# Delta rule on quarters of TensorE's array: the two halves taking turns, and turns by tokens as products with the unit matrix

## The chip, the cores and the metric

The kernel runs on one core of one Trainium2 chip. The metric is device time in microseconds (us) of one execution. A core has five engines that work side by side, each through its own queue of instructions in order: TensorE (PE in the profile; its weight loads are PEld), VectorE (DVE), ScalarE (ACT), GpSimd (POOL) and SyncE (SP), which issues the large transfers. They meet at semaphores.

## The reference

Two transformer-like layers run on 256 tokens of 1024 channels. The first has block attention, a pooling mixer, and a feed-forward part with a short convolution. The second has a convolution branch and an RWKV-7 branch side by side, and then a layer of 16384 small experts. The change is in the RWKV-7 branch: 8 heads of 64 channels, each with a 64 x 64 state that a delta rule updates token by token:

```python
    def step(state, inp):
        r_t, k_t, v_t, w_t, kk_t, a_t = inp
        sa = jnp.einsum('bhij,bhj->bhi', state, -kk_t)
        state = (state * w_t[:, :, None, :]
                 + sa[..., None] * (kk_t * a_t)[:, :, None, :]
                 + v_t[..., None] * k_t[:, :, None, :])
        y_t = jnp.einsum('bhij,bhj->bhi', state, r_t)
        return state, y_t
    ...
    mean = jnp.mean(y, axis=-1, keepdims=True)
    var = jnp.mean(jnp.square(y - mean), axis=-1, keepdims=True)
    y = ((y - mean) * lax.rsqrt(var + GN_EPS)).reshape(B, S, RWKV_CH) * gn_w.astype(F32) + gn_b.astype(F32)
```

## The kernel before

Activations lie with channels on the 128 partitions and tokens along the row. The large products (`linear`, lines 312 to 315) take weights of 128 x 128 in two parts, high and low, against 256 tokens in two parts: 24 matmuls for 1024 input channels. Weights come in pieces of 1 MB (`fetch`), ScalarE copies the high part (line 205) and VectorE subtracts the low part (line 207).

The RWKV branch is worked in four chunks of 64 tokens. A tile `m` of 128 partitions is two heads: partitions 0 to 63 and 64 to 127, the two halves. All products of one head with one chunk are 64 x 64 with 64 rows, so each uses one quarter of the array: the upper left one for the first half, the lower right one for the second. They are in plain fp32, which the trace shows as two records for each matmul.

`quads(f)` calls `f` for the eight pairs of a half `h` and an index `c` of 0 to 3. The result of a set of eight lands in one PSUM tile of two banks (`two_banks`), where `c // 2` is the bank and `c % 2` the place in it. Four functions use it:

- `heads(m)`, for m of 0 to 3, makes the matrices of the keys for the four chunks (line 1100) and inverts a triangular matrix for each of the eight pairs in five levels. A level has a set of eight products (line 1125), ScalarE's copy to `X` (line 1127), a second set (line 1131), VectorE's subtraction (line 1132) and VectorE's transpose (line 1134): 40 sets in all.
- `values2(m)` turns the values and the keys by tokens (`turn4`) and makes three products for each pair (line 1185): 24 matmuls in one call of `quads`, four calls.
- `chunks()` is the chain over the four chunks. Here `c` of `quads` is the tile `m`. A chunk has one product set for `G`, one for `U` and one for the next state `S`, and the output set `Y`, which has two matmuls for each pair from the second chunk on (line 1209). Two or three matmuls on zeros (`warm`, line 382) stand ahead of each set.
- `group_norm` normalises a chunk's output on VectorE and ScalarE and turns it with `turn4`.

`turn4` turns eight 64 x 64 blocks: in the first half as TensorE transposes (line 1144), in the second as products with the unit matrix (line 1146). There are 16 turns: four of `heads`, eight of `values2`, four of `group_norm`.

The heads' steps and the taps of the convolution branch (line 1287, on VectorE) are put between the projections by a small clock of due times (`at`, `tick`, `flow`). That sets the program's order. Within block 2 the compiler's scheduler then places the instructions of every engine by its own estimate of when each can run, so the order on an engine is not that of the text, and it changes when an instruction's estimated length changes.

Of the kernel before, what the change touches and what calls it, by code (L numbers as in the profile page):

```python
# [22 lines left out]
C = 64  # L23
# [150 lines left out]
class Kern:  # L174
# [711 lines left out]
    def quads(self, f):  # L886


        for h in range(2):
            for c in range(4):  # L890
                f(c, slice(64 * h, 64 * h + 64), c // 2, c % 2)

    def by4(self, p):

# [242 lines left out]
    def turn4(self, p, src):  # L1137

        te, ident = self.nc.tensor, self.c("ident")

        def turn(c, h, b, i):
            out = p[h, b, i * C:i * C + C]
            if h.start == 0:
                te.transpose(out, src(c, h), ident[h, h])
            else:
                te.matmul(out, src(c, h), ident[h, h], start=True, stop=True)

        self.quads(turn)

    def values2(self, m):  # L1150

# [554 lines left out]
```

## Time and profile before

| | |
|---|---|
| Runs before, median of 3 | 1444.72 us (1439.47 to 1444.98) |
| Profiled execution, own time | 1444.46 us |
| Its span, first to last instruction | 1442.7 us |
| PE busy over the span | 1400.3 us (97%) |
| DVE, ACT, POOL busy | 1110.6, 719.0, 269.6 us |
| Mean granted clock of TensorE | 0.979 of full speed (2.4 GHz) |

The first product on a quarter of the array starts at 447.4 us, the last at 586.3 us. Busy time of PE counts each matmul from its start to the modelled end of its pipeline; a matmul of the next instruction starts long before that, so 97% is not a share of what the array can do. What a stretch of matmuls costs is therefore read from starts in the timeline: merged rows give the first start and the time to the last end. A granted clock of 0.5 is the lower of TensorE's two levels, 1.2 GHz.

### The profile page before, as it was taken

To read this page: it belongs to the slowest core of one execution; us is meant where nothing else is said; L and a number is where in the kernel's file an instruction comes from. 1 tells how busy PE (TensorE), PEld (TensorE's weight loads), DVE (VectorE), ACT (ScalarE), POOL (GpSimd) and SP (SyncE) were. 2 spreads that over 40 slices of the span, in tenths; PEclk is the share of its full clock that TensorE was granted. 3 is DMA by queue.
4 is the path that set the end of the run, shared out by engine and by line. 5 is a ranking of instruction groups with operands and counts; after the bars stand their busy time and mean duration, and the time that the engine had idled before them with its cause. 6 is when DMAs were issued, how large, how long until landed. Compare 5 with 4: busy or idle time off the path is not lost. (4 is left out here: it accounts for less than half of the span.)

```text
span 1442.7 us, 27290 instructions
## 1 busy us (share of the span) xinstructions
PE 1400.3 (97%) x11208; PEld 1284.6 (89%) x11208; DVE 1110.6 (77%) x1967; ACT 719.0 (50%) x1079; POOL 269.6 (19%) x242
## 2 busy tenths in 40 slices
PE   9999999999869999989998999999999999999997
PEld 7889999999868897989998999999987777888886
DVE  5779999994598875769978867878679999655555
ACT  5576566564674333554453544434454444444443
POOL 1800032220285210022456440000000000000000
PEclk8999999999989998999999999999999999999999
DMA  7568867862413110364544555445555556654552
GB/s 282 196 199 295 295 220 266 273 221 88 161 59 112 37 60 2 117 212 168 179 172 147 205 175 176 164 160 176 172 209 174 187 199 230 206 201 175 196 184 88
DMA packets 40446, 253.83 MB, mean 176 GB/s; under 512 B 4736, under 2 KB 4992, under 8 KB 13440
## 3 DMA queue, kind: packets, MB, share of 16 engines
q1 hardware_dynamic: 38592, 246.79, 49.5%
q10 hardware_dynamic: 1728, 5.28, 1.1%
q8 instruction: 88, 1.44, 0.4%
q14 instruction: 38, 0.31, 0.1%
HBM read 249.96 MB, written 2.10 MB: 175 GB/s over the span
## 5 line engine op out<-in xcount | busy, mean ns | idle before, releaser
L205 ACT CAST whi<-raw 128x1024 fp32r<-128x1024 f32 (+1 forms) x418 | 435.1, 1043 | 498.5 <-PE psu L313 219.7
L207 DVE TENSOR_TENSOR wlo<-raw,whi 128x1024 fp32r<-128x1024 f32 (+1 forms) x389 | 488.3, 1259 | 197.1 <-ACT whi L205 196.1
L312 PE MATMUL psu<-u3hi,whi 128*128 128x256 f32 x1128 | 285.6, 286 | 4.4 <-DVE qe L520 4.4
L313 PE MATMUL psu<-u3lo,whi 128*128 128x256 f32 x1128 | 281.3, 283 | 0.0
L312 PEld LDWEIGHTS psu<-u3hi,whi 128*128 128x128 f32 x1128 | 214.5, 190 | 4.6 <-DVE qe L520 4.6
L313 PEld LDWEIGHTS psu<-u3lo,whi 128*128 128x128 f32 x1128 | 214.2, 190 | 0.0
L315 PE MATMUL psu<-u3hi,wlo 128*128 128x256 f32 x1128 | 180.9, 282 | 4.0 <-DVE wlo L207 2.9
L315 PEld LDWEIGHTS psu<-u3hi,wlo 128*128 128x128 f32 x1128 | 154.4, 189 | 5.2 <-DVE wlo L207 3.3
L1394 PE MATMUL acc<-whi,u3hi 128*128 128x512 f32 x504 | 140.8, 399 | 0.0
L1394 PE MATMUL acc<-whi,u3lo 128*128 128x512 f32 x504 | 138.2, 394 | 0.0
L1394 PE MATMUL acc<-wlo,u3hi 128*128 128x512 f32 x504 | 138.2, 394 | 0.0
L1394 PEld LDWEIGHTS acc<-wlo,u3hi 128*128 128x128 f32 x504 | 94.7, 188 | 22.3
L1394 PEld LDWEIGHTS acc<-whi,u3lo 128*128 128x128 f32 x504 | 94.7, 188 | 22.0
L1394 PEld LDWEIGHTS acc<-whi,u3hi 128*128 128x128 f32 x504 | 92.2, 188 | 19.1
L207 POOL TENSOR_TENSOR wlo<-raw,whi 128x1024 fp32r<-128x1024 f32 x29 | 72.0, 2483 | 190.5 <-ACT whi L205 190.5
L312 PE MATMUL mm<-u3hi,whi 128*128 128x256 f32 (+1 forms) x312 | 82.3, 295 | 0.0
L313 PE MATMUL mm<-u3lo,whi 128*128 128x256 f32 (+1 forms) x312 | 78.7, 284 | 0.0
L313 PE MATMUL mm<-flo,whi 128*128 128x256 f32 x272 | 67.6, 282 | 0.0
L312 PE MATMUL mm<-fhi,whi 128*128 128x256 f32 x272 | 67.6, 282 | 0.0
L312 PEld LDWEIGHTS mm<-u3hi,whi 128*128 128x128 f32 x312 | 59.5, 191 | 3.2 <-issue 2.5
L312 PE MATMUL mm<-n3hi,whi 128*128 128x256 f32 (+1 forms) x160 | 48.3, 326 | 14.0 <-DVE kr L960 9.4
L313 PEld LDWEIGHTS mm<-u3lo,whi 128*128 128x128 f32 x312 | 59.5, 191 | 0.3 <-issue 0.2
(432 smaller groups left out, 2599.4 us busy)
## 6 DMA issues: line engine op xcount, KB each, us to landing
raw<-in_w_fm SPq DMA_DIRECT2D x74, 1024.0 KB, 4.9
raw<-in_peer_u SPq DMA_DIRECT2D x64, 1024.0 KB, 4.8
raw<-in_peer_v SPq DMA_DIRECT2D x64, 1024.0 KB, 4.9
ada<-in_ada_w SPq DMA_DIRECT2D x40, 512.0 KB, 5.3
raw<-in_w_qkv SPq DMA_DIRECT2D x5, 1024.0 KB, 10.4
H<-in_ada_w SPq DMA_DIRECT2D x8, 512.0 KB, 3.9
raw<-in_w_qkv SPq DMA_DIRECT2D x4, 256.0 KB, 5.3
xd<-kr SPq DMA_DIRECT2D x1, 1024.0 KB, 9.9
```

What stands on the lines that cost most here:

```text
L205: self.nc.scalar.copy(hi, src)
L207: e.tensor_tensor(lo, src, hi.bitcast(F32), op=OP.subtract)
L312: mm(out, w[k][0], x[k][0], start=start and k == 0, stop=False)
L313: mm(out, w[k][0], x[k][1], start=False, stop=False)
L315: mm(out, w[k][1], x[k][0], start=False, stop=stop and k == n - 1)
L1394: mm(acc[a], w[:, tt * 128:tt * 128 + 128], v[:, dh * 512:dh * 512 + 512], start=start, stop=stop)
```

## The change

`quads` runs over the same eight pairs, but the halves take turns, and the second half is two indices ahead: (first, 0), (second, 2), (first, 1), (second, 3), (first, 2), (second, 0), (first, 3), (second, 1). So the two halves mostly write different banks. `turn4` has no transposes any more: both halves are products with the unit matrix.

```diff
     def quads(self, f):
 
 
-        for h in range(2):
-            for c in range(4):
-                f(c, slice(64 * h, 64 * h + 64), c // 2, c % 2)
+        for n in range(8):
+            h = n % 2
+            c = (n // 2 + 2 * h) % 4
+            f(c, slice(64 * h, 64 * h + 64), c // 2, c % 2)
...
-        def turn(c, h, b, i):
-            out = p[h, b, i * C:i * C + C]
-            if h.start == 0:
-                te.transpose(out, src(c, h), ident[h, h])
-            else:
-                te.matmul(out, src(c, h), ident[h, h], start=True, stop=True)
-
-        self.quads(turn)
+        self.quads(lambda c, h, b, i: te.matmul(p[h, b, i * C:i * C + C], src(c, h), ident[h, h], start=True, stop=True))
```

The count of instructions stays: 680 matmuls on quarters, 10388 in all. Line numbers of the changed kernel are one higher from line 892 to `turn4`, and six lower after it. The scheduler moves instructions on PE, DVE and ACT; POOL's and SP's order stays. Groups of quarter products between full-size ones are 51 where they were 50.

In the first levels of `heads` PE has, before (1125 and 1131 are the two sets of a level, `keep` is the unit matrix, 312 to 315 are projections):

```order
L1125 MATMUL two<-lora,Alv 64x64 x8
L312 MATMUL mm<-n3hi,whi 128x256
L313 MATMUL mm<-n3lo,whi 128x256
L312 MATMUL mm<-n3hi,whi 128x256
L1125 MATMUL two<-lora,Alv 64x64 x8
L1144 MATMUL two<-keep,beb_4547 64x64 x4
L1146 MATMUL two<-keep,beb_4547 64x64 x4
L313 MATMUL mm<-n3lo,whi 128x256
L312 MATMUL mm<-n3hi,whi 128x256
L1131 MATMUL two<-eL,X 64x64 x8
L313 MATMUL mm<-n3lo,whi 128x256
L1131 MATMUL two<-eL,X 64x64 x8
```

And with the change:

```order
L1126 MATMUL two<-lora,Alv 64x64 x8
L1109 MATMUL sm<-bonus,cst 128x256
L1126 MATMUL two<-lora,Alv 64x64 x8
L1142 MATMUL two<-keep,beb_4547 64x64 x8
L1132 MATMUL two<-eL,X 64x64 x16
L312 MATMUL mm<-n3hi,whi 128x256
L313 MATMUL mm<-n3lo,whi 128x256
```

The single projections between the sets move behind them, and the turn is eight products of one kind.

In the chain over the chunks VectorE has, before (1218 copies half of `U`, which PE needs for the next state; 1345 is the reciprocal of the convolution branch's norm):

```order
L1224 TENSOR_TENSOR G<-two,sg 128x256
L1261 TENSOR_TENSOR Y<-Y,ysm 128x256
L1345 RECIPROCAL cvr<-cvr 128x256
L1264 TENSOR_REDUCE ysm<-yq 128x4
L1218 COPY U<-two 128x128
```

And with the change:

```order
L1218 TENSOR_TENSOR G<-two,sg 128x256
L1255 TENSOR_TENSOR Y<-Y,ysm 128x256
L1258 TENSOR_REDUCE ysm<-yq 128x4
L1212 COPY U<-two 128x128
L395 RECIPROCAL ysm<-ysm 128x4
L1260 TENSOR_TENSOR Y<-Y,ysm 128x256
L1339 RECIPROCAL cvr<-cvr 128x256
```

The reciprocal stood ahead of the copy of `U` and now stands behind it.

## Rows read from the trace of the kernel before

**Rows 1.** The profile's page, busy time of each engine over the span

```profile
PE 1400.3 (97%) x11208; PEld 1284.6 (89%) x11208; DVE 1110.6 (77%) x1967; ACT 719.0 (50%) x1079; POOL 269.6 (19%) x242
```

**Rows 2.** Busy time by stretch: PE, PEld, DVE, ACT, POOL, granted clock, DMA share

```profile
420.00:440.00 20.00, 14.68 (x80) 14.24 (x81) 18.95 (x27) 13.33 (x24) 15.53 (x16) 0.66 0.15 54
440.00:543.00 103.00, 101.60 (x1318) 91.92 (x1316) 81.93 (x169) 37.40 (x78) 28.39 (x32) 1.00 0.18 63
543.00:590.00 47.00, 45.00 (x460) 37.17 (x460) 28.29 (x76) 17.52 (x38) 1.50 (x2) 0.85 0.07 24
560.00:580.00 20.00, 18.40 (x164) 15.08 (x164) 10.11 (x29) 7.70 (x16) 0.00 (x0) 0.66 0.00 1
```

**Rows 3.** Waits of PE, 440 to 500: us in total, times, longest

```profile
PE two L1125 <- DVE lora L1120: 1.2, 2, 1.1
```

**Rows 4.** Waits of DVE, 440 to 500

```profile
DVE lora L1120 <- POOL eL L1118: 4.1, 4, 1.3
DVE eL L1132 <- PE two L1131: 3.1, 5, 1.2
DVE cvy L952 <- PE mm L315: 1.9, 1, 1.9
```

**Rows 5.** Waits of DVE, 500 to 543

```profile
DVE eL L1132 <- PE two L1131: 7.0, 5, 2.4
DVE QE L1173 <- PE sm L1170: 3.1, 2, 2.8
```

**Rows 6.** Timeline of PE, 407.8 to 408.4: start, us to the last end

```profile
408.15 0.38 PE L1015 MATMUL two<-lr,lora 64*128 64x256 f32 x1
408.15 0.38 PE L1016 MATMUL two<-lr,lora 64*128 64x256 f32 x1
408.37 0.38 PE L1015 MATMUL two<-lr,lora 64*128 64x256 f32 x1
```

**Rows 7.** Timeline of PE, 512.6 to 513.4, where one set follows another

```profile
512.70 0.22 PE L1125 MATMUL two<-lora,Alv 64*64 64x64 f32 x1
512.75 0.22 PE L1185 MATMUL two<-kp,QE 64*64 64x64 f32 x1
512.76 0.22 PE L1125 MATMUL two<-lora,Alv 64*64 64x64 f32 x1
...
513.05 0.34 PE L1185 MATMUL two<-kp,QE 64*64 64x64 f32 x3
```

**Rows 8.** Timeline of PE, a turn and sets of a level, 447 to 478

```profile
447.36 0.41 PE L1144 MATMUL two<-keep,beb 64*64 64x64 f32 x4
447.70 0.68 PE L1146 MATMUL two<-keep,beb 64*64 64x64 f32 x8
...
471.31 1.54 PE L1131 MATMUL two<-eL,X 64*64 64x64 f32 x32
473.09 0.96 PE L1131 MATMUL two<-eL,X 64*64 64x64 f32 x16
475.49 2.46 PE L1125 MATMUL two<-lora,Alv 64*64 64x64 f32 x48
```

**Rows 9.** Busy time by stretch of line 1125, line 1131 (440 to 500) and line 1185

```profile
440.00:500.00 60.00, 12.69 (x240) 11.38 (x240) 1.00 0.21 72
440.00:500.00 60.00, 11.84 (x224) 10.55 (x224) 1.00 0.21 72
500.00:520.00 20.00, 2.83 (x48) 2.69 (x48) 1.00 0.16 54
```

**Rows 10.** Timeline of all engines, 559 to 563, in the chain

```profile
559.68 1.75 DVE L1345 RECIPROCAL cvr<-cvr 128x256 f32<-128x256 f32 x1 [1.05 <-ACT cvr L1344]
561.63 0.28 DVE L1218 COPY U<-two 128x128 f32<-128x128 f32 x1
561.96 0.49 PE L382 MATMUL two<-zero 128*128 128x256 bf16 x3 [1.60 <-DVE U L1218]
562.38 0.96 PE L1209 MATMUL two<-U,tb 64*64 64x64 f32 x16
```

## The prediction

> **What bounds the kernel now.** I read the page's busy times first, then a table by stretch, the waits of PE and of DVE in the stretch that holds the quarter products, and last the timeline of PE there. PE is busy 97% of the span [rows 1], so a saving on PE is worth something wherever PE does not wait. The reader should see where that holds: from 440 to 543 us PE is busy 101.6 of 103 us at the full clock, 2.4 GHz, with DVE at 81.9 [rows 2], and PE's only wait of note is 1.2 us [rows 3]. Just before, from 420 to 440, it is the other way round: DVE is busy 18.95 of 20 us, PE 14.68, and the granted clock averages 0.66 [rows 2]. From 440 on DVE waits for PE instead: 5.0 us up to 500, mostly on the second set of a level [rows 4], and 10.1 us from 500 to 543 [rows 5]. So PE sets the pace of heads and values, with DVE not far behind. From 543 to 590, the chain over the chunks, neither is full (45.0 and 28.3 of 47 us) [rows 2]; there results go round between PE, ACT and DVE.
>
> **What two halves do at once.** The trace already has places where matmuls of the two halves stand side by side. Lines 1015 and 1016 read the upper and the lower 64 rows, alternate in program order, and start together: two at 408.15, and the next 0.22 us later [rows 6]. For quarters, the end of one set beside the start of the next shows it: the second half's last records of line 1125 at 512.70 and 512.76 with the first half's record of line 1185 at 512.75 between them [rows 7]. Within one half a record follows the other after 0.06 us ((0.34 - 0.22) / 2, the three records at 513.05 [rows 7]). So two records, one of each half, take the 0.06 us that one takes now. With strict turns nearly a whole set should run so, where today only about three records at each border do.
>
> **Part 1: the 40 sets of the levels.** A set is 16 records and takes 0.96 us alone, two 1.54, three 2.46 [rows 8]. As eight pairs it takes seven steps of 0.06, one first step that is 0.05 longer, and the 0.22 of the last record: 0.69. Two sets take 15 steps, 1.17; three take 23, 1.65. The savings are 0.27, 0.37 and 0.81, per set 0.27, 0.19 and 0.27. I take 0.25: 40 x 0.25 = 10.0 us of PE. Of 640 records 464 lie before 500 us [rows 9], so 7.3 fall there and 2.7 after.
>
> **Part 2: the 24 products of each of the four calls of values.** Such a call is 48 records and takes 2.83 us [rows 9]. By turns of three matmuls it would be 23 steps and 0.27, 1.65 us, if TensorE takes the other half's matmuls while one half has two in hand, as the border at 512.7 suggests. 1.2 x 4 = 4.8 us, all after 500.
>
> **Part 3: the turns.** Now four transposes start at 447.36, and the second half's products start only at 447.70 and end 0.68 later, at 448.38 [rows 8]. As 16 records in pairs the turn should take the 0.69 of a set, so it ends at 448.05: 0.33 saved, four times before 500 (1.3), eight up to 543 (2.6), four in the chain (1.3). A rule speaks against this part. The Trainium skill, "Perfetto Trace Analysis", section Transposes, says that a logical transpose should be a transpose and not a standard matmul, since it skips the arithmetic. The rows agree in that four transposes take 0.41 and four products 0.68. By that rule 16 turns would cost 16 x 0.27 = 4.3 us more instead of 5.2 less, and the sum below would lose 9 of its PE time. I do not follow it, since the second half's products now stand behind the first half's and would stand beside them.
>
> **What of it shows, 440 to 543.** PE would need 7.3 + 1.3 = 8.6 us less before 500, and 2.7 + 4.8 + 2.6 = 10.1 less after. What DVE can give is its waits on PE: 5.0 before 500 and 10.1 after [rows 4, 5]; its 4.1 us of waits on POOL stay [rows 4]. The lower of the two in each piece is 5.0 and 10.1, 15.1 us. That is the most, if each wait vanishes and no new one comes. The least is nothing, if DVE's order binds at once. With both engines nearly full and results passing back and forth, some of either's time is lost in new waits; I take three quarters, 11.3 us. What is late next is DVE: 81.9 us of work against some 92 us of stretch.
>
> **The chain, 543 to 590.** It has eleven single sets, three double ones (16 matmuls, 32 records) and four turns. Singles save 0.27 each (3.0). A double saves 16 steps of 0.06 less the three that its halves share at their border today, 0.78 each (2.3). Turns 1.3. Together 6.6 us of PE time, of which I count half, 3.3, because sets stand both on the round of results and beside it (PE's waits for ACT and DVE take the rest). To that comes the moved reciprocal: it holds DVE for 1.75 us from 559.68, the copy of U ends behind it, and PE waits 1.60 for U [rows 10]. In the new order it stands behind that copy, so 1.6 us go. Against it stands the clock: from 560 to 580 the granted clock averages 0.66, so 20 x 0.34 / 0.5 = 13.6 us at the lower level, 1.2 GHz, at a place where PE had idled [rows 2, 10]. With shorter sets PE is idle for a larger share. If the lower level lasts as long again, it costs 6.8 us of full-clock work; bounds are 0 and 6.8, and I take 1.0, as at the lower level a set in pairs takes about what a set takes now at the upper. The chain gives 3.3 + 1.6 - 1.0 = 3.9 us.
>
> **The other edits.** One more group of quarter products (51 for 50) means two more switches between quarter and full-size matmuls. No row shown has a switch alone; the nearest is the step from transposes to products inside a turn, from 447.36 + 0.41 - 0.22 = 447.55 to 447.70, 0.15 us [rows 8]. Two cost between nothing and 0.3; I take 0.1, within the rounding. POOL's and SP's order stays. After 590 nothing changes, and PE is the engine that is full there too, so what is gained is carried to the end.
>
> **Sum.** 11.3 + 3.9 = 15.2 us. From the profiled execution's 1444.46 us (span 1442.7 and 1.8 around it, 0.3 below the median of the runs, 1444.72) that is 1429.3; I say 1429.
>
> **Rivals.**
> *PE's saving shows in full.* If DVE's overlapping instructions leave it more room than its busy time says, all of 8.6 + 10.1 + 6.6 + 1.6 = 26.9 us go: 1418. For it: DVE's instructions start before the previous one's end. Against: DVE was the late engine until 440.
> *DVE takes over at once.* Taps and low parts stand in DVE's order between the steps of the levels; where PE is early it waits behind them. Then 440 to 543 gives 4 and the chain 2: 1438.5. For it: DVE at 80% and the backlog from before 440. Against: it waited 15 us on PE.
> *The clock falls in the levels: slower.* If PE's waits on DVE between 440 and 543 become like those from 420 to 440 (5.3 idle in 20 us, clock 0.66), each 20 us loses 20 x 0.34 = 6.8 us of full-clock work. Three such stretches cost 20.4: 1449.7, slower than before. It decides from 15.2 / 6.8 = 2.2 stretches on. Against: PE's idle share by the sum is under 10 of 92 us. The Trainium skill, "TensorE: Matmul & The Clock Gate", section "A second HAM failure mode", describes just such a throttling through short idle times between groups of matmuls; here 440 to 543 runs at 1.00 with groups as short as eight matmuls.
> *The halves do not run side by side.* Then the sets stay, and turns lose 16 x 0.27 = 4.3 less the hole of some 0.1 ahead of the second half (1.6): 1447. Rows 6 and 7 speak against it.
>
> **How the numbers follow.** Forecast 0.57, PE in full 0.16, DVE at once 0.17, clock 0.05, no turns 0.05. The forecast's own range is 1422 to 1436. What a measurement can tell from no change is 0.5%, 7.2 us: faster means below 1437.2 or so. Forecast 0.56 faster and 0.01 same; PE in full 0.16 faster; DVE at once 0.07 faster, 0.10 same; clock 0.02 same and 0.03 slower; no turns 0.03 same and 0.02 slower. Faster 0.79, same 0.16, slower 0.05. The range, 1418 to 1440, leaves out half of PE in full, a sixth of DVE at once and nearly all of the last two: 0.2.
>
> **What would show it.** Right: a set of 16 records merged in under 0.75 us where it took 0.96; a call of values near 1.65; a turn near 0.7 with no hole; DVE's waits on line 1131's sets mostly gone; the last quarter product before 574. Wrong: records of the two halves that start 0.06 apart instead of together (no turns); PE waits on DVE of more than 8 us from 440 on (DVE at once); a granted clock below 0.9 between 440 and the start of the chain (clock).

## The result and the profile after

The changed kernel takes 1421.73 us, median of 6 runs (1417.35 to 1423.11), where the kernel before took 1440.03 beside it on the same chip (6 runs, 1439.47 to 1444.98). The ratio is 0.9857, 95% interval 0.9835 to 0.9878: 20.6 us less by the ratio, 18.3 by the medians. Forecast were 1429.0 us and 15.2 us less. So the change made the kernel faster as forecast, inside the range, by 5 us more than the sum had it (3 by the medians); and the gain sits elsewhere than the sum put it, which is the matter of this text.

The page of the kernel after has PE's busy time 31 us below [rows 1]. It still fills 97% of the span:

```profile
span 1417.0 us, 27418 instructions
...
PE 1369.4 (97%) x11272; PEld 1258.2 (89%) x11272; DVE 1111.3 (78%) x1967; ACT 718.8 (51%) x1079; POOL 270.7 (19%) x242
```

To see where the time went, I cut each trace at three marks: the first quarter product, the last record of the values, and the last turn by tokens. Between the first two lie heads and values ("the head" below), between the last two the chain. Busy time by stretch, of the kernel before: the first 40 us, head, chain, and the piece of the chain at the lower clock (us, then PE, PEld, DVE, ACT, POOL, granted clock, DMA share, GB/s):

```profile
0.00:40.00 40.00, 37.14 (x173) 29.96 (x174) 22.07 (x43) 21.00 (x33) 7.68 (x13) 0.87 0.74 275
447.40:542.40 95.00, 93.60 (x1251) 84.34 (x1251) 75.10 (x155) 32.16 (x68) 28.39 (x32) 1.00 0.16 57
542.40:586.30 43.90, 41.90 (x437) 33.85 (x435) 26.05 (x71) 16.68 (x36) 1.50 (x2) 0.84 0.03 7
563.50:577.20 13.70, 13.70 (x103) 10.98 (x101) 5.76 (x17) 5.71 (x13) 0.00 (x0) 0.50 0.01 2
```

The same of the kernel after, with two short pieces of its head:

```profile
0.00:40.00 40.00, 36.97 (x192) 29.71 (x192) 27.32 (x51) 24.88 (x39) 12.82 (x19) 1.00 0.86 320
442.20:528.50 86.30, 79.06 (x1298) 70.91 (x1297) 76.63 (x157) 31.77 (x68) 29.26 (x32) 0.96 0.19 63
528.50:560.30 31.80, 29.79 (x454) 23.95 (x452) 25.01 (x70) 16.86 (x36) 1.45 (x2) 1.00 0.04 7
469.60:473.00 3.40, 3.40 (x37) 3.17 (x39) 3.40 (x9) 0.23 (x1) 0.17 (x1) 0.50 0.00 0
496.90:500.30 3.40, 3.40 (x52) 3.06 (x51) 3.40 (x8) 0.78 (x3) 0.00 (x0) 0.50 0.26 39
```

The head gave 8.7 us (95.0 to 86.3) and the chain 12.1 (43.9 to 31.8). What follows the chain is the same length: 1442.7 - 586.3 = 856.4 before, 1417.0 - 560.3 = 856.7 after. The remaining 5.2 us of the two spans' difference lie ahead of the first quarter product (447.4 to 442.2): the profiled execution of before has a piece at the lower clock in its first 40 us (0.87), that of after has none. The change touches nothing there, and an experiment with the same code up to that point, the kernel before with the reciprocal cut, has no such piece and its first quarter product at 442.3; so it is not counted as the change's. 8.7 + 12.1 - 0.3 = 20.5, the 20.6 of the ratio.

The steps themselves are what the sum said. Timeline of PE after, two sets of line 1132 (line 1131 before) and the last turn:

```profile
464.15 1.15 PE L1132 MATMUL two<-eL,X 64*64 64x64 f32 x32
...
468.82 0.68 PE L1132 MATMUL two<-eL,X 64*64 64x64 f32 x16 [2.98 <-DVE eL L1133]
...
471.55 2.38 PE L1126 MATMUL two<-lora,Alv 64*64 64x64 f32 x48
...
559.87 0.68 PE L1142 MATMUL two<-keep,Y 64*64 64x64 f32 x16
560.48 0.39 PE L313 MATMUL mm<-u3lo,whi 128*128 128x256 f32 x1
```

A set of 16 records takes 0.68 us for 0.96 [rows 8] (forecast 0.69), two sets 1.15 for 1.54 (1.17), a turn 0.68 without a hole for 1.02 (0.69). The 48 records at 471.55 take 2.38, where 1.65 was forecast, since they run at the clock of 0.50 up to 473.0. For two calls of the values, 96 records (line 1179; 1185 before):

```profile
500.00:520.00 20.00, 3.46 (x96) 3.29 (x96) 0.99 0.27 102
```

1.73 us a call for 2.83 [rows 9], where 1.65 was forecast. So the halves do run beside each other, for as long as a whole set.

What PE no longer needs it partly waits for. Waits of PE, kernel after, 440 to 500 us (us in total, times, longest), which answer to [rows 3]:

```profile
PE two L1132 <- DVE eL L1133: 4.7, 2, 3.0
PE two L1126 <- DVE lora L1121: 2.3, 2, 1.4
PE two L1126 <- DVE eL L1133: 0.2, 1, 0.2
```

7.2 us instead of 1.2. The largest is the 2.98 at 468.82 above; DVE's timeline just before it, kernel after:

```profile
464.74 0.95 DVE L1281 SCALAR_TENSOR_TENSOR cvacc<-cvy,vec,cvacc 128x256 f32<-128x256 f32 x1
465.72 0.42 DVE L1091 TENSOR_TENSOR beb<-av,eN 64x256 f32<-64x256 f32 x1
...
466.91 1.52 DVE L1281 SCALAR_TENSOR_TENSOR cvacc<-cvy,vec,cvacc 128x256 f32<-128x256 f32 x3
468.35 0.75 DVE L1133 TENSOR_TENSOR eL<-eL,two 128x256 f32<-128x256 f32 x2
```

The two sets end at 465.30, and the subtraction that empties them (line 1133) starts at 468.35: three taps of the convolution (line 1281) and what is queued before them stand between, without a gap. On the other side DVE's waits for PE shrink. Waits of DVE, kernel after, 440 to 500, for [rows 4]:

```profile
DVE lora L1121 <- POOL eL L1119: 4.6, 4, 1.3
DVE eL L1133 <- PE two L1132: 1.5, 2, 1.2
DVE cvy L953 <- PE mm L315: 0.5, 1, 0.5
```

And from 500 to 529, for [rows 5]:

```profile
DVE eL L1133 <- PE two L1132: 1.6, 1, 1.6
DVE QE L1167 <- PE sm L1164: 0.5, 1, 0.5
```

5.0 became 2.0 and 10.1 became 2.1.

### The profile page after: what moved, and what is told of

It is laid out like the page before. It is cut to its first block, busy times and chain, and to the rows that moved or that the text cites. A ratio compares the mean times of both kernels' runs of the same rounds, so it can differ in the third digit from the quotient of the medians.

```text
span 1417.0 us, 27418 instructions
## 1 busy us (share of the span) xinstructions
PE 1369.4 (97%) x11272; PEld 1258.2 (89%) x11272; DVE 1111.3 (78%) x1967; ACT 718.8 (51%) x1079; POOL 270.7 (19%) x242
```

## The experiments

Three theories went in, A, B and C in the expectations. The first is the prediction's: the shorter sets and turns are the gain, in the head up to what DVE can give, and in the chain with the wait for U gone. The second: it is the end of the transposes that keeps the clock up in the chain. The third: in the head DVE has become the bound, and what relieves DVE there gives more. All results in one table; head and chain are cut at the same marks as above, in one execution of each kernel, and "low" is the time at the granted clock of 0.50 in each. Each ratio is to executions of the kernel before beside that run.

| run | ratio to before | head us | low | chain us | low |
|---|---|---|---|---|---|
| before | 1 | 95.0 | 0 | 43.9 | 13.7 |
| after | 0.9857 (0.9835 to 0.9878) | 86.3 | 6.8 | 31.8 | 0 |
| order only | 0.9943 (0.992 to 0.9965) | 94.5 | 3.4 | 36.6 | 0 |
| turns only | 0.9945 (0.9927 to 0.9962) | 95.4 | 3.4 | 37.0 | 0 |
| after, fewer taps | 0.981 (0.9789 to 0.983) | 82.1 | 0 | 33.3 | 3.4 |
| before, fewer taps | 0.9992 (0.998 to 1.0005) | 95.4 | 0 | 44.0 | 13.7 |
| before, reciprocal cut | 0.9948 (0.9926 to 0.997) | 95.1 | 0 | 37.1 | 0 |
| after, one bank | 0.9861 (0.9838 to 0.9884) | 86.4 | 6.8 | 31.9 | 0 |
| after, one warming matmul | 0.9876 (0.984 to 0.9912) | 84.9 | 3.4 | 37.5 | 6.8 |
| after, taps off DVE | 0.9925 (0.9898 to 0.9951) | 93.4 | 10.2 | 32.1 | 0 |
| after, reciprocal cut | 0.9858 (0.9837 to 0.9878) | 86.5 | 6.8 | 31.9 | 0 |
| after, low parts on POOL | 0.991 (0.9894 to 0.9927) | 91.6 | 10.2 | 33.9 | 3.4 |
| after, both of these | 0.9919 (0.99 to 0.9937) | 91.5 | 10.2 | 32.4 | 0 |
| after, again | 0.984 (0.9818 to 0.9862) | 86.4 | 6.8 | 31.8 | 0 |

**The new order alone.** The kernel before with `quads` of the kernel after; turns stay transposes in the first half and products in the second.

```diff
-        for h in range(2):
-            for c in range(4):
-                f(c, slice(64 * h, 64 * h + 64), c // 2, c % 2)
+        for n in range(8):
+            h = n % 2
+            c = (n // 2 + 2 * h) % 4
+            f(c, slice(64 * h, 64 * h + 64), c // 2, c % 2)
```

> Halves take turns in quads; the turns by tokens keep transposes in the first half, as before. Theory A (the gain is the side-by-side run of the two halves): 40 sets, values and the chain's sets gain as in the changed kernel (a set 0.68 us), turns lose their 16 x 0.33 = 5 us of PE time; 1424 to 1430 where before is 1440 and the changed kernel 1421. Theory B (the transposes are what hurts: they break the row of products and the clock falls in the chain): 1432 to 1438, with a stretch at 1.2 GHz in the chain again. Theory A expects no such stretch only if density is the cause; it leaves that open.

It took 1435.46 us (ratio 0.9943): slower than theory A's range, and in the range of the second theory (B), but without the stretch at 1.2 GHz in the chain that B forecast. Next to nothing of the gain comes from the head (94.5 for 95.0); the chain gives it (36.6 for 43.9). Timeline of PE, a set and a turn of this kernel:

```profile
462.08 0.68 PE L1126 MATMUL two<-lora,Alv 64*64 64x64 f32 x16
462.69 0.24 PE L1145 MATMUL two<-keep,beb 64*64 64x64 f32 x1
462.86 0.33 PE L1147 MATMUL two<-keep,beb 64*64 64x64 f32 x2
463.12 0.24 PE L1145 MATMUL two<-keep,beb 64*64 64x64 f32 x1
...
464.14 0.33 PE L1147 MATMUL two<-keep,beb 64*64 64x64 f32 x2
464.40 0.38 PE L313 MATMUL mm<-n3lo,whi 128*128 128x256 f32 x1
```

The sets have their 0.68, but the turn now runs from 462.69 to 464.47, 1.78 us for 1.02 [rows 8]. Each step between a transpose and a product takes 0.17 to 0.26 us from start to start, and nothing runs beside it. Twelve turns in the head lose 12 x 0.76 = 9.1 us, most of what sets and values save on PE there (12.7 us: the 16.8 found below, less 12 x 0.34 for the turns). Of the 3.6 us left, the 3.4 us at the lower clock take up to 1.7, and PE's idle time in the head grows by 1.4.

**The turns alone.** The kernel after with the order of before.

```diff
-        for n in range(8):
-            h = n % 2
-            c = (n // 2 + 2 * h) % 4
-            f(c, slice(64 * h, 64 * h + 64), c // 2, c % 2)
+        for h in range(2):
+            for c in range(4):
+                f(c, slice(64 * h, 64 * h + 64), c // 2, c % 2)
```

> Turns by tokens are products with the unit matrix in both halves; quads keeps its old order, all of the first half and then the second. Theory A: a turn takes the 0.96 us of a set where it took 1.02, so nothing is gained or lost: 1438 to 1442, sets still 0.96 us. Theory B (transposes hold the clock down in the chain): the stretch at 1.2 GHz from 563 to 577 goes and with it 6.8 us: 1432 to 1435. By the rule that products cost more than transposes: 1444.

1433.48 us (0.9945), again nothing in the head, with 3.4 us of it at the lower clock. The time is the one that B forecast. Timeline of PE, its first turn:

```profile
447.40 0.96 PE L1141 MATMUL two<-keep,beb 64*64 64x64 f32 x16
448.30 0.39 PE L313 MATMUL mm<-n3lo,whi 128*128 128x256 f32 x1
```

0.96 for 1.02: products in place of transposes cost nothing even in the old order, since the hole between the two kinds goes with them. All that this kernel wins it wins in the chain (37.0, none of it at the lower clock). Its order of DVE is another there: the long reciprocal stands behind the copy of U, as in the kernel after, and PE has no wait for U.

The two parts alone win 0.5 and -0.4 us in the head, together 8.7. Neither showed a gain in it without the other; the lower clock hides up to 1.7 us of each.

**Fewer taps on DVE, after and before.** Both leave out 28 of the 30 taps that this loop adds for one of the convolution's four tiles, some 10 us of DVE in the head.

```diff
-        for j in range(30):
+        for j in range(2 if m == 1 else 30):
```

> The changed kernel with 28 of the 30 VectorE taps of one of the convolution's four channel tiles left out (the one whose taps run between 450 and 500 us): DVE has 28 x 0.4 = 11 us less to do there, PE the same. Theory C (after the change DVE sets the pace of the levels): the stretch from the first quarter product to the last product of values, 86.3 us, gets 5 us shorter or more, and the time falls by 4 to 9 us. Theory D (PE still sets the pace, or the round of results): less than 2 us.

> The kernel before with the same 28 taps left out. Theory C (PE set the pace of the levels before): 0 to 2 us faster than before, the stretch of 95.0 us stays above 93. Theory D (DVE or the round of results set it already): the same gain as in the changed kernel with these taps left out.

In the kernel after the head goes to 82.1, 4.2 less where theory C asked for 5 or more, and the time to 1415.67; in the kernel before nothing moves (0.9992). (The profiled execution of after with fewer taps is the slowest of its four, 1421.16; it has 10.2 us at the lower clock in its first 40.) The head's row of after with fewer taps:

```profile
447.50:529.60 82.10, 76.83 (x1300) 68.51 (x1299) 66.01 (x129) 31.79 (x68) 28.93 (x32) 1.00 0.19 66
```

And of before with fewer taps:

```profile
445.20:540.60 95.40, 94.12 (x1251) 84.69 (x1251) 65.14 (x129) 32.18 (x68) 27.50 (x32) 1.00 0.17 57
```

DVE's 10 us are worth nothing before and 4.2 us after: 2.0 as less idle time of PE (7.2 to 5.3), and 2.2 as PE's work, all at the full clock here. PE's row at the full clock, 76.83, tells what its saving in the head is: 93.60 - 76.83 = 16.8 us. The rest of the head of after follows: its idle time grew from 1.4 to 7.2 us (86.30 - 79.06), which takes 5.8, and the two pieces at 0.50 make its work 2.2 longer (79.06 - 76.83): 16.8 - 5.8 - 2.2 = 8.8. In the chain of the fewer-taps kernel the reciprocal stands ahead of the copy of U again, PE waits 1.9 us for it, and 3.4 us run at the lower clock: 33.3 for 31.8.

**The reciprocal in four pieces, in the kernel before.** DVE can do other work between the pieces.

```diff
-        nc.vector.reciprocal(rs, rs)
+        for i in range(0, T, 64):
+            nc.vector.reciprocal(rs[:, i:i + 64], rs[:, i:i + 64])
```

> The kernel before with the convolution norm's reciprocal of 256 columns cut into four of 64, so that only the first, about 0.45 us, stands ahead of the copy of U that PE waits for. Theory E (the stall of 1.75 us on DVE is what idles PE, and the clock falls behind it): the stretch at 1.2 GHz in the chain goes, the chain shrinks from 43.9 to 36 or 37 us, 1433 to 1436, as with the turns alone. Theory B (the transposes hold the clock down): only the 1.3 us of the stall go, the stretch at 1.2 GHz stays, 1438 to 1441.

1435.5 us (0.9948, 7.5 us less), with the same products and transposes as before; some full-size products and DVE's list behind the copy of U stand in another order. Its chain by stretch:

```profile
537.40:574.50 37.10, 36.04 (x436) 29.42 (x435) 25.89 (x74) 16.93 (x36) 1.50 (x2) 1.00 0.04 9
```

and DVE's timeline in it:

```profile
555.12 0.36 DVE L1264 TENSOR_REDUCE ysm<-yq 128x4 f32<-128x256 f32 x1
555.40 0.28 DVE L1218 COPY U<-two 128x128 f32<-128x128 f32 x1
555.60 0.54 DVE L1346 RECIPROCAL cvr<-cvr 128x64 f32<-128x64 f32 x1
```

The copy of U slips in between two pieces, PE's wait for it falls from 1.6 to 0.4, and the clock stays at 1.00 where it had been 0.50 for 13.7 us. Chain 43.9 to 37.1. The transposes are all there, as they are in the order alone, and so the second theory is not needed for the clock.

**Both halves into one bank.** In the kernel after the two halves work at the same time on different banks of PSUM; here on the same one, in its other 64 partitions.

```diff
-            c = (n // 2 + 2 * h) % 4
+            c = n // 2
```

> The changed kernel without the second half's offset of two indices (c = n // 2): both halves of a pair write the same PSUM bank at the same time, on different partitions. If the bank can take two halves' results at once: a set stays 0.68 us and the time 1418 to 1423. If it makes them take turns: a set goes back toward 0.96 us, and the time to 1430 or more.

No difference: ratio 0.9861, and a set, from the timeline of PE:

```profile
529.73 0.68 PE L1203 MATMUL two<-sg,eL 64*64 64x64 f32 x16
```

The Trainium skill, "TensorEngine Tiling (Array Packing)", section Restrictions and Gotchas, says that different row tiles can't access the same PSUM bank at once. This trace shows no cost of it, 0.68 us for a set on one bank as on two, for two halves that write different partitions; the measurement decides. So the offset of two in `c` isn't where the gain comes from.

**One warming matmul instead of three** ahead of each set of the chain that waits (line 382 multiplies zeros).

```diff
-WARM_CHAIN = 3
+WARM_CHAIN = 1
```

> The changed kernel with one matmul on zeros ahead of each set of the chain instead of three. Theory F (they lie in waits, and the chain's round of results sets the pace): within 1 us of the changed kernel, unless the clock falls in the chain, which costs up to 7 us. Theory G (the chain is bound by PE's own row of matmuls now): 14 sets x 0.22 = 3 us faster.

The chain is 37.5 us for 31.8. Its second half by stretch:

```profile
545.00:565.00 20.00, 17.70 (x213) 15.40 (x209) 13.47 (x36) 13.74 (x22) 0.00 (x0) 0.83 0.13 45
```

6.8 us of it at the lower clock, and PE waits 1.9 us for Y. The time as a whole, 0.9876, can't be told from that of the kernel after, and with one profile it is not shown that the missing zeros brought the lower clock. The head, which the edit leaves alone, shows something else. PE and DVE have the same instructions in the same order there as in the kernel after, and PE the same waits (4.7 us for line 1133), but only the first of the two pieces at 0.50:

```profile
442.20:527.10 84.90, 77.60 (x1297) 69.48 (x1297) 76.65 (x157) 31.77 (x68) 29.22 (x32) 0.98 0.18 64
```

It is 1.4 us shorter than 86.30, and PE's busy time is less by as much (79.06 to 77.60): so the second piece costs the head 1.4 us, and its coming is not settled by the order and the waits.

**One tile's taps from DVE to ScalarE and POOL.** Following the third theory, without leaving anything out.

```diff
-TAPS_ACT = (2,)
+TAPS_ACT = (2, 1)
```

> The changed kernel with the taps of the channel tile that VectorE works between 450 and 500 us given to ScalarE (products) and GpSimd (sums) instead. Theory C (DVE sets the pace of the levels after the change): DVE's 12 us go as in the run without them, and the time falls by 3 to 7 us, to 1414 to 1418. Rival: GpSimd, which makes the masked matrices of each level, is late instead, as 30 sums of 0.7 us come into its queue: 1421 or slower.

A loss: 1430.48 us (0.9925), head 93.4. Busy time from 460 to 480:

```profile
460.00:480.00 20.00, 13.56 (x181) 11.87 (x180) 9.82 (x19) 11.12 (x25) 19.06 (x25) 0.82 0.11 47
```

and the largest wait of PE in the head:

```profile
PE two L1126 <- POOL cvacc L1293: 6.9, 3, 4.4
```

DVE is down to 9.82 of 20 us, but POOL, which adds these taps (line 1293) and also prepares the matrices of the keys, is at 19.06. PE waits for POOL instead, as the rival had it.

The chain of this kernel has the changed products, but DVE has the long reciprocal ahead of the copy of U, as in the kernel before. PE's wait for U and the chain by stretch:

```profile
PE two L382 <- DVE U L1212: 1.9, 1, 1.9
535.60:567.70 32.10, 29.81 (x454) 23.48 (x451) 24.34 (x69) 16.62 (x36) 1.50 (x2) 1.00 0.04 7
```

32.1 us, only 0.3 more than in the kernel after, and the clock stays at 1.00.

**The reciprocal in four pieces, in the kernel after** (the diff is that shown above).

> The changed kernel with the convolution norm's reciprocal cut into four of 64 columns. In the changed kernel it stands behind the copy of U already, and PE waits 1.0 us for a later result behind it. Theory E (the gain of the chain's order is used up): within 1.5 us of the changed kernel. Rival (the reciprocal still holds the chain): 2 us faster or more.

1421.68 us (0.9858): nothing more to win, since the copy of U already stands ahead. With the same cut on both sides the chain is 37.1 with the old products and 31.9 with the new, so sets and turns are worth 5.2 us of it once that cut is made.

**A quarter of the low parts of this stage to POOL.** Two subtractions of weights (line 207) leave DVE for POOL in the head.

```diff
-LO_SECOND = 0
+LO_SECOND = 0.25
```

> The changed kernel with every fourth low part of the weights in block 2 made on GpSimd instead of VectorE (2.5 us there, 1.3 on VectorE). Theory C (DVE sets the pace of the levels): DVE has some 4 us less between 442 and 528, the heads' and values' stretch shrinks from 86.3 by 2 to 4 us, time 1417 to 1420 beside the changed kernel's 1421.5. Rival: GpSimd delays the levels' masked matrices by 2.5 us each time, and the stretch grows.

1429.02 us (0.991), head 91.6, where theory C forecast 2 to 4 us less than 86.3. Its head also begins 3.6 us later (445.8 for 442.2). PE's largest wait in the head:

```profile
PE two L1132 <- DVE eL L1133: 7.0, 2, 4.3
```

Two subtractions fewer on DVE (2.6 us), and yet DVE is busy for 77.2 us in the head, as it was (76.6), and PE waits longer for it, 7.0 us for 4.7 at the same line. 10.2 us of the head ran at the lower clock for 6.8. Which of these is the larger part, and what made them, stays open; the rival, POOL late by these subtractions, isn't what PE's waits show.

**Both, cut reciprocal and low parts.**

> Both of these edits on the changed kernel. If they add up, theory C gives 1416 to 1419. Otherwise as the low parts alone.

1429.61 us (0.9919), as the low parts alone.

**The changed kernel once more,** beside the last ones.

> The changed kernel itself, beside the other three on the same chip: 1421 (1417 to 1423). Also a second profile of it: if the chain's 31.9 us and the heads' 86.3 come again within 0.5 us, and no stretch at 1.2 GHz lies in the chain, the split of the gain stands on the order and not on one execution.

1418.75 us (0.984, interval 0.9818 to 0.9862). The head by stretch repeats to 0.1 us, the low clock in it too:

```profile
442.20:528.60 86.40, 79.11 (x1298) 70.90 (x1297) 76.64 (x157) 31.77 (x68) 29.20 (x32) 0.96 0.18 63
```

No kernel that leaves nothing out came out faster than the changed one.

## Why the prediction was right, and where it was not

**The steps.** Sets 0.68 and 1.15 (0.69 and 1.17 forecast), turns 0.68 (0.69), calls of values 1.73 (1.65): the 0.06 us between two records of one half, read from the border of two sets [rows 7] and from lines 1015 and 1016 [rows 6], was enough to price them. PE's saving in the head is 16.8 us at the full clock, of 18.7 counted for 440 to 543. This part was shown by the timelines.

**What shows in the head: too much counted.** 11.3 us were taken, three quarters of what DVE waited for PE; 8.7 came. DVE is late next, as written: PE's 7.2 us of waits in the head are nearly the 8 that were named as the sign of "DVE at once", and fewer taps bring 4.2 us back, while before they brought none. The term left out is the clock: 2.2 us of PE's work went to two pieces at 0.50 that begin 0.8 and 1.5 us after PE has waited 2.98 and 1.70 us for line 1133. The second of them cost the head 1.4 us, as the kernel with one warming matmul shows; what the first cost, with DVE busy for 3.40 of its 3.40 us, no run shows. That rival was priced as 20 us stretches with a mean of 0.66, and its sign, a mean below 0.9 ahead of the chain, did not come (0.96); pieces of 3.4 us did.

**The chain: the step that was mis-sized.** 3.9 us were forecast, 12.1 came. Its three terms:

- Sets and turns: half of 6.6 us of PE time, 3.3. Measured 5.2, by the same cut reciprocal with old and new products (37.1 and 31.9). So most of what they save stood on the round of results, not beside it.
- The reciprocal behind the copy of U: 1.6. The order did change so, and the wait for U is gone, but others stand in its place. PE's waits in the chain of the kernel after:

```profile
PE two L382 <- DVE yq L1265: 1.0, 1, 1.0
PE two L382 <- DVE S L1232: 0.6, 1, 0.6
```

With 0.3 for another result they are 1.9 us, as before (1.6 and 0.3). With the taps off DVE the reciprocal stands ahead again, and the chain is 0.3 longer. So this term by itself was worth some 0.3.
- The clock: -1.0. I carried the 13.6 us at 1.2 GHz over into the new chain and asked only what they would cost in it, though the time before had them already. They went altogether, and 13.7 us at half the clock are 6.9 us of work.

The cut reciprocal takes 6.8 us from the old chain, about what the lower clock costs, and then the new products take 5.2: 12.0 together. But the new products with the reciprocal still ahead reach 32.1 (taps off DVE), 11.8 less. In the four kernels where the sets take turns and PE waits 1.9 us for U (order alone, fewer taps, taps off DVE, low parts on POOL), 0 or 3.4 us are left of the 13.7. So either of the two can take away all or most of the lower clock, and these runs do not say which did it in the kernel after.

Rows that could have told it stood ahead of the forecast: a PE wait of 1.60 us for U at 561.96 [rows 10], and a mean clock of 0.66 from 560 to 580 [rows 2]. I had noted that the clock fell "at a place where PE had idled" and took the idling away in another sentence, without joining the two.

**What was luck.** That the time came within 8 us of the forecast is in part two errors of opposite sign: the head 2.6 us too much, the chain 8.2 too little. Some 6.8 us of the chain's gain are a clock that was booked as a loss.

**The rivals.** PE's saving in full, 26.9 us, is not what happened (20.6), nor is DVE at once (6). The halves run side by side. A turn as products takes 0.96 us in the old order for 1.02 with transposes in one half, and in the new order 0.68 for 1.78. The Trainium skill, "Perfetto Trace Analysis", section Transposes, says that a transpose should be used and not a standard matmul. That did not pay here for turns that share themselves between transposes and products; a turn of eight transposes was not run.

**Open.** Why the clock falls in one chain and not in another is not settled. In the order alone PE waits 1.9 us for U, longer than before, and the clock stays, as it does with the taps off DVE:

```profile
PE two L382 <- DVE U L1219: 1.9, 1, 1.9
```

(waits of PE, order only, in the chain). With fewer taps and with the low parts on POOL the same wait stands in a chain with 3.4 us at 0.50, in the kernel before 1.6 us are followed by 13.7. So in the old chain it was enough to take the wait away, but the wait isn't by itself enough to cause. Not settled either is what the two pieces in the head hang on beyond PE's waits: with the same order and the same waits one execution has two of them and another, with one warming matmul, has one. Of the kernels with both parts of the change, only that with fewer taps, where PE's longest wait for line 1133 is 1.5 us, has none there.

## What to carry to other kernels

Where two halves of the array work on independent small products, write them by turns, and make all of a group the same kind of instruction; in the head either alone gave next to nothing here, both together 8.7 us. When an engine that sets the pace gets lighter, look at what stands in the next engine's list between the steps that it is waiting for; here, of 17 us on PE, about half showed. And where a stretch already runs at the lower clock, price its going as a term of its own: here it was worth some 6.8 us, more than the sets and turns of that stage, and it went, all or most of it, with the shorter products as well as with the wait ahead of it.

## What the runs showed of the hardware that I had not expected

- A step between a transpose and a product on quarters costs 0.17 to 0.26 us from start to start, where the products of the two halves go at 0.06 us from pair to pair. A turn of four transposes and four products in alternation took 1.78 us, as products 0.68.
- Two halves that write one PSUM bank at the same time, in different partitions, run as fast as on two banks (0.68 us a set; ratios 0.9861 and 0.9857).
- One reciprocal of 128x256 takes 1.75 us [rows 10], and four of 128x64 take 0.54 each, 2.2 together, with other instructions let in between: in the kernel before the cut cost DVE 0.4 us and saved 7.5.
